# A transformer block with expert retrieval on one core: a fourth gather buffer, rows turned step by step, whole ada tiles, norms by inverse root

## The chip, the core and the metric

The kernel runs on one core of a Trainium2 chip. Its engines run side by side, each through its own instructions in order: TensorE (PE in the profile; PEld is its weight load), VectorE (DVE), ScalarE (ACT), GpSimd (POOL) and SyncE (SP), which only issues DMAs here. DMA queues: q1 carries what SyncE issues, q10 what ScalarE issues, q0 what GpSimd issues (the gathers). The metric is the device time of one execution in microseconds (us), as the median of several runs. A profiled execution is one more run, taken with the hardware profiler.

## The reference

One block of a streaming encoder, 512 tokens of 2048 features, all in fp32:

```python
mod = jax.nn.silu(c) @ ada_w[l] + ada_b[l]
sh1, sc1, gt1, sh2, sc2, gt2 = [m[:, None, :] for m in jnp.split(mod, N_ADA, axis=-1)]
h = rmsnorm(x, norm1_g[l]) * (1.0 + sc1) + sh1
x = x + gt1 * token_mixer(h, ...)
h = rmsnorm(x, norm2_g[l]) * (1.0 + sc2) + sh2
x = x + gt2 * peer_ffn(h, ...)
return rmsnorm(x, final_norm_g)

def rmsnorm(x, g):
    y = x * lax.rsqrt(jnp.mean(x * x, axis=-1, keepdims=True) + EPS)
    return y * g

def peer_ffn(h, w_q, sub_keys, u_tab, v_tab):
    ...
    act = jax.nn.gelu(jnp.einsum('td,tkd->tk', h_b, u_tab[i_b]))
    return jnp.einsum('tk,tkd->td', g_b * act, v_tab[i_b])
```

In `peer_ffn` eight heads pick 16 of 16384 experts each (`idx`, with weights `g`). So each token uses 128 experts, rows of two tables u and v of 16384 x 2048.

## The kernel before

**First half.** `ada_lead` multiplies silu(c) into the shift and scale columns of `ada_w`. It loads tiles `araw` of 128 x 1024 floats, six buffers, on SyncE, and accumulates them into `adacc` on VectorE (line 201), a few of them on TensorE (`prow`). It does so in five pieces of columns (`PIECES`), and the input projection of a piece (`plk`, `plead`, `pgl`) begins when its h is made (`h_hi`, `h_lo`, lines 257 to 259). A weight tile `raw` is split by ScalarE and VectorE into `hi` and `lo`, and three matmuls (lines 129 to 131) make one product. `rstd_from` (line 211) makes the inverse root of a mean square: a square root on ScalarE, a reciprocal on VectorE, one Newton step. It serves four norms of 128 x 512: the first, the two small ones of the attention ranks, and the second (`rs2`).

**Expert half.** Tokens 176 to 511 (336 of them, `TD`) go through all 16384 experts densely: 128 chunks of 128 experts, in 32 groups of four. For a chunk, `u_chunk` makes `pu` (two weight tiles `raw<-in_u_t`, 48 matmuls), a gelu, and `make_w` multiplies by the routing weights `gg` and `gl`, read back from DRAM (`g_d`, `gl_d`), into `wh` and `wl`. `v_slice` then multiplies with the v rows into `pvv` (two tiles `raw<-in_v_t`, 48 matmuls), and VectorE adds that to `acc` (line 1207). The first 32 chunks have their `pu` made earlier (`lead_chunk`, while routing runs) and kept in DRAM (`act_d`): these "old" groups come last and have only v matmuls.

**Gathered tokens.** Tokens 0 to 127 and 48 more gather their rows instead: `fetch` (line 984) starts an indirect DMA of 128 rows of 8 KB into a buffer `gt` (tag "gat"); VectorE multiplies it with h (`use_u`, line 990) or adds it to a sum (`use_v`, lines 1000 and 1002). The 48 are two sets, x (32 tokens) and y (16), laid out so that each gather fills 128 partitions; `build_h` lays out their h by four copies, sixteen transposes and four evacuations (`h2r` and `ph2x`, `h2s` and `ph2y`). There are 352 gathers. `gather_to` starts them at a steady rate per sub-step (`sub`: 16 in a group with u and v, 8 in an old one), each tied to the last matmul placed ahead of it:

```python
if len(landing) == GLAG:
    use_one()
landing.append((use, fetch(tab, ix, k), k, args, post))
```

`x_done` runs after the last gather of set x: it stores `accs["x"]` to `gx_d` and calls `build_h("y")`, whose result takes the same buffer (tag "hX", one buffer).

**Order.** A scheduler places each engine's instructions by priority, mostly in the order in which the code is written; `hi` and `lo` are raised. SyncE issues all weight tiles, ada tiles and gg loads in one order, and a DMA that waits for its buffer holds those behind it.

## Time and profile before

| | |
|---|---|
| median of 3 runs | 3721.33 us (3717.72 to 3724.13) |
| the profiled execution | 3719.46 us, span 3717.7 us |
| TensorE busy | 3568.5 us (96%) |
| VectorE busy | 2887.9 us (78%) |
| ScalarE busy | 1360.4 us (37%) |
| DMA | 962.75 MB, mean 259 GB/s |
| q1 / q0, share of 16 DMA engines' span | 42.5% / 26.6% |

Busy time is a sum over stages with different limits, so the table by itself doesn't say where time can be saved. A wait is read as "who waited <- who ended it". Idle time counts for the kernel's end only where it is on the engine that the stage waits for. The granted clock is the share of TensorE's full speed (2.4 GHz) that it was given over a stretch: it has two levels, 1.2 and 2.4 GHz.

### The profile page before, as it was taken

How to read it: one execution, taken by the hardware profiler on the slowest of the kernel's cores; microseconds unless marked ns; L12 is line 12 of the kernel's file. 1: busy time of each engine (PE TensorE's matmuls, PEld its weight loads, DVE VectorE, ACT ScalarE, POOL GpSimd, SP SyncE). 2: the span in 40 equal slices, each digit the busy share in tenths (PEclk: the TensorE clock that was granted, in tenths of full speed). 3: DMA queues.
4: the chain of work that ended last, by engine and by line, in shares of the span. 5: the costliest groups of instructions: out<-in, count | busy, mean ns of one | idle time of the engine just before them, and what ended most of it. 6: DMA issues, size and time to landing. Idle time of an engine off the chain costs nothing.

```text
span 3717.7 us, 52118 instructions
## 1 busy us (share of the span) xinstructions
PE 3568.5 (96%) x20165; PEld 3207.0 (86%) x20165; DVE 2887.9 (78%) x4315; ACT 1360.4 (37%) x1942; POOL 488.2 (13%) x399
## 2 busy tenths in 40 slices
PE   7999999999999989999999999999998999998888
PEld 4776778888788878889999999999998999998878
DVE  7866675455344348999988999999898998999877
ACT  3243335555422234235653333333333333332233
POOL 0000000000000000000112222222222222223400
PEclk9999999999999999999999999999999999999999
DMA  9746655544444443246789999999998999999874
GB/s 307 251 142 205 194 182 167 162 158 146 129 145 136 137 121 97 90 138 212 288 327 371 369 375 372 383 374 376 368 377 325 377 366 358 371 380 354 311 271 147
DMA packets 280824, 962.75 MB, mean 259 GB/s; under 512 B 25672, under 2 KB 76872, under 8 KB 233424
## 3 DMA queue, kind: packets, MB, share of 16 engines
q1 hardware_dynamic: 203184, 533.84, 42.5%
q0 software_dynamic: 52272, 391.14, 26.6%
q10 hardware_dynamic: 25120, 34.44, 2.7%
q8 instruction: 158, 2.59, 0.3%
q14 instruction: 90, 0.74, 0.1%
HBM read 913.26 MB, written 46.01 MB: 258 GB/s over the span
## 4 chain that ended last, share of the span: by engine, by line
PE 75%; DVE 14%; DMA 8%; issue 2%; ACT 1%; ACTq 0%; DVEq 0%; SPq 0%; POOLq 0%
PE pvv L129 6%; PE pvv L131 6%; PE pvv L130 6%; PE pu L131 5%; PE pu L130 5%; PE pu L129 5%; PE proj L129 4%; PE proj L131 4%; PE proj L130 4%; DVE lo L115 2%; DMA raw<-in_u_t 2%; PE pbr L131 2%; PE pbr L129 2%; PE pbr L130 2%; DMA raw<-in_v_t 2%
## 5 line engine op out<-in xcount | busy, mean ns | idle before, releaser
L129 PE MATMUL pvv<-wh,hi 128*128 128x336 f32 x2048 | 653.9, 319 | 39.2 <-DVE acc L1207 37.5
L131 PE MATMUL pvv<-wh,lo 128*128 128x336 f32 x2048 | 654.2, 319 | 2.5 <-DVE lo L1316 2.5
L130 PE MATMUL pvv<-wl,hi 128*128 128x336 f32 x2048 | 654.2, 319 | 0.0
L114 ACT ACTIVATE hi<-raw 128x1024 fp32r<-128x1024 f32 x288 | 304.6, 1059 | 576.3 <-PE pu L130 179.6
L129 PE MATMUL pu<-h2c_hi,hi 128*128 128x336 f32 x1536 | 487.8, 318 | 13.6 <-ACT hi L114 7.0
L131 PE MATMUL pu<-h2c_hi,lo 128*128 128x336 f32 x1536 | 489.6, 319 | 8.7 <-DVE lo L115 8.6
L130 PE MATMUL pu<-h2c_lo,hi 128*128 128x336 f32 x1536 | 487.5, 317 | 0.0
L129 PEld LDWEIGHTS pvv<-wh,hi 128*128 128x128 f32 x2048 | 389.4, 190 | 46.7 <-issue 36.9
L1315 ACT ACTIVATE hi<-raw 128x1024 fp32r<-128x1024 f32 x256 | 271.1, 1060 | 427.1 <-PE pu L130 176.1
L117 ACT ACTIVATE hi<-raw 128x1024 fp32r<-128x1024 f32 (+2 forms) x193 | 201.8, 1046 | 594.0 <-PE proj L130 164.2
L115 DVE TENSOR_TENSOR lo<-raw,hi 128x1024 fp32r<-128x1024 f32 x288 | 350.8, 1218 | 61.4 <-ACT hi L114 53.7
L131 PEld LDWEIGHTS pvv<-wh,lo 128*128 128x128 f32 x2048 | 391.4, 191 | 5.2 <-DVE lo L1316 5.0
L130 PEld LDWEIGHTS pvv<-wl,hi 128*128 128x128 f32 x2048 | 389.8, 190 | 0.0
L984 POOL DMA_INDIRECT gt<-in_u,idx x128 | 160.9, 1257 | 1703.1 <-PE pg L1091 1318.2
L118 DVE TENSOR_TENSOR lo<-raw,hi 128x1024 fp32r<-128x1024 f32 (+2 forms) x193 | 232.7, 1206 | 155.9 <-ACT hi L117 146.3
L1316 DVE TENSOR_TENSOR lo<-raw,hi 128x1024 fp32r<-128x1024 f32 x256 | 311.8, 1220 | 28.8 <-ACT hi L1315 28.3
L1002 DVE SCALAR_TENSOR_TENSOR acca<-gt,wk,acca 128x2048 f32<-128x2048 f32 x127 | 297.9, 2346 | 19.4 <-DMA gt<-in_v,idx 19.2
L990 DVE SCALAR_TENSOR_TENSOR gt<-gt,h2nat 128x2048 f32<-128x2048 f32 x128 | 292.5, 2287 | 24.3 <-DMA gt<-in_u,idx 23.8
L129 PEld LDWEIGHTS pu<-h2c_hi,hi 128*128 128x128 f32 x1536 | 290.5, 189 | 15.3 <-ACT hi L114 8.3
L131 PEld LDWEIGHTS pu<-h2c_hi,lo 128*128 128x128 f32 x1536 | 290.1, 189 | 12.8 <-DVE lo L115 12.7
L160 DVE SCALAR_TENSOR_TENSOR adacc<-raw,silc,adacc 128x512 f32<-128x512 f32 x240 | 180.0, 750 | 143.5 <-DMA raw<-in_ada 139.7
L130 PEld LDWEIGHTS pu<-h2c_lo,hi 128*128 128x128 f32 x1536 | 290.7, 189 | 0.0
(357 smaller groups left out, 7206.0 us busy)
## 6 DMA issues: line engine op xcount, KB each, us to landing
raw<-in_u_t SPq DMA_DIRECT2D x256, 512.0 KB, 7.6
raw<-in_v_t SPq DMA_DIRECT2D x256, 512.0 KB, 7.5
raw<-in_ada SPq DMA_DIRECT2D x128, 512.0 KB, 4.0
araw<-in_ada SPq DMA_DIRECT2D x64, 512.0 KB, 6.3
raw<-in_w_gate SPq DMA_DIRECT2D x44, 512.0 KB, 3.7
g_d<-stg POOLq DMA_DIRECT2D x10, 2048.0 KB, 10.6
gg<-g_d SPq DMA_DIRECT2D x16, 1280.0 KB, 17.3
raw<-in_w_out SPq DMA_DIRECT2D x32, 512.0 KB, 4.5
```

The costliest lines, as they stand in the source:

```text
L114: SC.activation(hi[:, :n], raw[:, :n], AF.Copy)
L115: VE.tensor_sub(lo[:, :n], raw[:, :n], hi[:, :n])
L117: SC.activation(hi[:, :n], raw[:, :n], AF.Copy)
L118: VE.tensor_sub(lo[:, :n], raw[:, :n], hi[:, :n])
L129: TE.matmul(out, w[0], x[0], start=first, stop=False, **kw)
L130: TE.matmul(out, w[0], x[1], start=False, stop=False, **kw)
L131: last_mm[0] = TE.matmul(out, w[1], x[0], start=False, stop=last, **kw)
L160: VE.scalar_tensor_tensor(acc[:], r, silc[:, j:j + 1], acc[:], op0=ALU.mult, op1=ALU.add)
L990: pace(VE.scalar_tensor_tensor(t[:], t[:], 1.0, h()[:], op0=ALU.mult, op1=ALU.mult, accum_out=dt[:, k:k + 1]), mybir.DependencyClass.NoSync)
L1002: ins = VE.scalar_tensor_tensor(accs[nm][:], t[:], w[:, k:k + 1], accs[nm][:], op0=ALU.mult, op1=ALU.add)
L1315: SC.activation(hi[:], raw[:], AF.Copy)
L1316: VE.tensor_sub(lo[:], raw[:], hi[:])
```

## The change

Five edits. `NGAT` goes from 3 to 4 and `GLAG` from 2 to 3: four gather buffers, and a gather is read three gathers after it was started instead of two. `build_h` becomes a generator `h_steps`, one of whose five steps runs per lead chunk (set x) or per sub-step (set y, after six sub-steps of nothing). The ada tiles come from a copy of the same weights laid out tile by tile (`ada_l`), so a tile is one contiguous 512 KB. `rstd_from` takes the inverse root on ScalarE and has no reciprocal; the final norms in `scale_out` are left as they are. `load_g` loads the routing weights of one group where it loaded those of two, into buffers half as large.

```diff
--- before.py
+++ after.py
@@ -39,8 +39,8 @@
 M0 = 1
 PIECES = [(0,2),(2,4),(4,8),(8,12),(12,16)]
 NEG = -3.0e38
-NGAT = 3
-GLAG = 2
+NGAT = 4
+GLAG = 3
 NEARLY = 20
 CI, CT, CM, CR, CO, CF = 0, 128, 256, 384, 512, 640
 NCONST = 641
@@ -178,6 +178,9 @@
         VE.tensor_add(mod[:, v, 4 * q:4 * q + 4], pst[:, 0:4], adab[:, v, 4 * q:4 * q + 4])
         yield
 
+    def lead_tile(d0, d1, u):
+        return 2 * d0 + u
+
     def ada_lead(d0, d1, pool, sil2, npe):
         w = (d1 - d0) * 128
         cols = slice(d0 * 128, d1 * 128)
@@ -188,7 +191,7 @@
             acc = ap.tile([128, 512], F32, name="adacc", tag="adacc", bufs=2)
             for u in range(16 // nj):
                 raw = pool.tile([128, 1024], F32, name="araw", tag="araw", bufs=NARAW)
-                SY.dma_start(raw[:].rearrange("p (j c) -> p j c", j=nj), a["ada"][v, :, nj * u:nj * u + nj, cols])
+                SY.dma_start(raw[:], a["ada_l"][v, lead_tile(d0, d1, u)])
                 for jj in range(nj):
                     j = nj * u + jj
                     r = raw[:, jj * w:jj * w + w]
@@ -211,8 +214,7 @@
 
     def rstd_from(pss, out, n, tmp):
         VE.tensor_scalar(tmp[0], pss, 1.0 / n, EPS, op0=ALU.mult, op1=ALU.add)
-        SC.activation(tmp[1], tmp[0], AF.Sqrt)
-        VE.reciprocal(out, tmp[1])
+        SC.activation(out, tmp[0], AF.Abs_reciprocal_sqrt)
         VE.scalar_tensor_tensor(tmp[0], tmp[0], -0.5, out, op0=ALU.mult, op1=ALU.mult)
         VE.tensor_mul(tmp[0], tmp[0], out)
         VE.scalar_tensor_tensor(out, tmp[0], 1.5, out, op0=ALU.add, op1=ALU.mult)
@@ -772,7 +774,7 @@
             SC.activation(sq[:], x1T[:, d, :], AF.Square)
             if d == 15:
                 warm = Op.tile([128, 1], F32, name="warm")
-                SC.activation(warm[:], sq[:, 0:1], AF.Sqrt)
+                SC.activation(warm[:], sq[:, 0:1], AF.Abs_reciprocal_sqrt)
             VE.tensor_add(ssum[:], ssum[:], sq[:])
     VE.scalar_tensor_tensor(a2[:], mod[:, 4, :], 1.0, g2, op0=ALU.add, op1=ALU.mult)
     for d in range(6):
@@ -1004,21 +1006,36 @@
 
     hx = {}
 
-    def build_h(nm, tmp, psum):
+    def h_steps(nm, tmp, psum):
         r0, n = sets[nm][0:2]
         hx[nm] = gr.tile([128, D], F32, name="h2" + nm, tag="hX", bufs=1)
-        for j in range(4):
+
+        def copy(j):
             h2r = tmp()
             src = h2xT[:, 4 * j:4 * j + 4, None, r0:r0 + n].to_broadcast([128, 4, 128 // n, n])
             pin(VE.tensor_copy(h2r[:].rearrange("p (i q t) -> p i q t", i=4, t=n), src))
+            return h2r
+
+        def turn(j, h2r):
             pb = psum()
             for i in range(4):
                 pin(TE.transpose(pb[:, i * 128:i * 128 + 128], h2r[:, i * 128:i * 128 + 128], ident))
             SC.activation(hx[nm][:, j * 512:j * 512 + 512], pb[:], AF.Copy)
 
+        h2r = copy(0)
+        for j in range(4):
+            yield
+            turn(j, h2r)
+            if j < 3:
+                h2r = copy(j + 1)
+
+    later = []
+
     def x_done():
         SC.dma_start(gx_d[:], accs["x"][:])
-        build_h("y", lambda: Ep_[0].tile([128, 512], F32, name="h2s"), lambda: psu_[0].tile([128, 512], F32, name="ph2y", tag="pu", bufs=2))
+        gen = h_steps("y", lambda: Ep_[0].tile([128, 512], F32, name="h2s"),
+                      lambda: psu_[0].tile([128, 512], F32, name="ph2y", tag="pu", bufs=2))
+        later.extend([None] * 6 + [gen] * 5)
 
     Ep_, psu_ = [None], [None]
     gat = [("u", idx, k, use_u, (lambda: h2nat, dots, wk, g0), None) for k in range(128)]
@@ -1105,7 +1122,9 @@
             nb += 1
         gather_to(NEARLY * (c - NL0 + 1) // (NLEAD - NL0))
         if c == NL0 + 5:
-            build_h("x", lambda: Gp.tile([128, 512], F32, name="h2r", tag="h2r", bufs=2), lambda: bank("ph2x"))
+            hgen = h_steps("x", lambda: Gp.tile([128, 512], F32, name="h2r", tag="h2r", bufs=1), lambda: bank("ph2x"))
+        if c >= NL0 + 5:
+            next(hgen, None)
     PO.close("Gp")
     PO.close("Rp")
     PO.close("ps")
@@ -1137,19 +1156,21 @@
         steps[0] += 1
         if fin[0] is not None:
             next(fin[0], None)
+        if later:
+            gen = later.pop(0)
+            if gen is not None:
+                next(gen, None)
         gather_to(NEARLY + -(-(len(gat) - NEARLY) * steps[0] // (nsub - 33)))
 
     def load_g(g):
-        if g % 2:
-            return
-        t = Ep.tile([128, NW, 256], F32, name="gg", tag="gg", bufs=2)
-        tl = Ep.tile([128, 8 * WL], F32, name="gl", tag="gl", bufs=2)
-        SY.dma_start(t[:], g_d[:, :, 128 * g:128 * g + 256].rearrange("b p c -> p b c"))
-        SY.dma_start(tl[:], gl_d[:, 4 * WL * g:4 * WL * (g + 2)])
-        gtiles[g // 2] = t, tl
+        t = Ep.tile([128, NW, 128], F32, name="gg", tag="gg", bufs=2)
+        tl = Ep.tile([128, 4 * WL], F32, name="gl", tag="gl", bufs=2)
+        SY.dma_start(t[:], g_d[:, :, 128 * g:128 * g + 128].rearrange("b p c -> p b c"))
+        SY.dma_start(tl[:], gl_d[:, 4 * WL * g:4 * WL * (g + 1)])
+        gtiles[g] = t, tl
 
     def make_w(e2, at, tie=False):
-        g, c = divmod(e2, 8)
+        g, c = divmod(e2, 4)
         t, tl = gtiles[g]
         av = at[:, :32 * NW].rearrange("p (b t) -> p b t", t=32)
         ins = VE.tensor_mul(av, av, t[:, :, c * 32:c * 32 + 32])
@@ -1370,6 +1391,14 @@
     col = lambda n: f(n).reshape(-1, 128).T
     o["vecs"] = c(np.concatenate([f("c").reshape(128, 16), adab, col("norm1_g"), col("norm2_g"), col("mla_q_norm_g"),
                                   col("mla_kv_norm_g")], axis=1))
+    ada = f("ada_w")[0].reshape(128, 16, 6, 2048)
+    tiles = []
+    for d0, d1 in PIECES:
+        w = (d1 - d0) * 128
+        nj = 1024 // w
+        p = ada[:, :, 0:2, d0 * 128:d1 * 128].reshape(128, 16 // nj, nj, 2, w)
+        tiles.append(p.transpose(3, 1, 0, 2, 4).reshape(2, 16 // nj, 128, 1024))
+    o["ada_l"] = c(np.concatenate(tiles, axis=1))
     o["ada"] = c(f("ada_w")[0].reshape(128, 16, 6, 2048).transpose(2, 0, 1, 3))
     o["ada_b"] = c(f("ada_b").reshape(1, -1))
     w = f("w_in")[0]
```

Three places show how the order of instructions moves. The first is VectorE at the second norm; `n` and `rs` are the mean square and its inverse root, `hn` and `h_lo` the first chunks of the normed rows. Before:

```order
L776 TENSOR_TENSOR ssum<-ssum,sqo 128x512
L213 TENSOR_SCALAR n_9671<-pss_9668 128x512
L215 RECIPROCAL rs_9670<-n_9672 128x512
L216 SCALAR_TENSOR_TENSOR n_9671<-n_9671,rs_9670 128x512
L217 TENSOR_TENSOR n_9671<-n_9671,rs_9670 128x512
L218 SCALAR_TENSOR_TENSOR rs_9670<-n_9671,rs_9670 128x512
L257 SCALAR_TENSOR_TENSOR hn<-x1T,a_88,rs_9670 128x512 x2
L259 SCALAR_TENSOR_TENSOR h_lo<-hn,mod,h_hi 128x512 x2
```

After:

```order
L778 TENSOR_TENSOR ssum<-ssum,sqo 128x512
L216 TENSOR_SCALAR n_9668<-pss_9665 128x512
L218 SCALAR_TENSOR_TENSOR n_9668<-n_9668,rs_9667 128x512
L219 TENSOR_TENSOR n_9668<-n_9668,rs_9667 128x512
L220 SCALAR_TENSOR_TENSOR rs_9667<-n_9668,rs_9667 128x512
L259 SCALAR_TENSOR_TENSOR hn<-x1T,a_88,rs_9667 128x512 x2
L261 SCALAR_TENSOR_TENSOR h_lo<-hn,mod,h_hi 128x512
```

The reciprocal is gone, and the first `h_lo` stands after two `hn` as it did.

The second is VectorE in the expert half, where set y's h is laid out; `h2s` are the copies, `acca` a gather's use, `lo` the weight tiles. Before:

```order
L1162 TENSOR_TENSOR wl<-at,wh 128x336
L1013 COPY h2s<-h2xT 128x512
L1002 SCALAR_TENSOR_TENSOR acca<-gt,wk,acca 128x2048
L1013 COPY h2s<-h2xT 128x512
L1316 TENSOR_TENSOR lo<-raw,hi 128x1024
L1013 COPY h2s<-h2xT 128x512
L1207 TENSOR_TENSOR acc<-acc,pvv 128x672
L1013 COPY h2s<-h2xT 128x512
L1207 TENSOR_TENSOR acc<-acc,pvv 128x672
L1002 SCALAR_TENSOR_TENSOR acca<-gt,wk,acca 128x2048
L1316 TENSOR_TENSOR lo<-raw,hi 128x1024
```

After:

```order
L1016 COPY h2s<-h2xT 128x512
L1228 TENSOR_TENSOR acc<-acc,pvv 128x672
L1183 TENSOR_TENSOR wl<-at,wh 128x336
L1004 SCALAR_TENSOR_TENSOR acca<-gt,wk,acca 128x2048
L1337 TENSOR_TENSOR lo<-raw,hi 128x1024
L1016 COPY h2s<-h2xT 128x512
L1228 TENSOR_TENSOR acc<-acc,pvv 128x672
L1016 COPY h2s<-h2xT 128x512
L1337 TENSOR_TENSOR lo<-raw,hi 128x1024
L1004 SCALAR_TENSOR_TENSOR acca<-gt,wk,acca 128x2048 x2
L115 TENSOR_TENSOR lo<-raw,hi 128x1024
L1016 COPY h2s<-h2xT 128x512
```

The four copies stood within seven rows, with one weight tile and one gather's use among them. Now they span twelve, with three weight tiles and three uses, and all of it stands six sub-steps after the end of set x's sum.

The third is SyncE at the start of the expert half's main loop; `gg` and `gl` are the routing weights, `raw` the weight tiles. Before:

```order
L1147 DMA gg<-g_d 128x10x256
L1148 DMA gl<-gl_d 128x128
L109 DMA raw<-in_u_t 128x1024 x2
L1147 DMA gg<-g_d 128x10x256
L1313 DMA raw<-in_v_t 128x1024 x2
L1148 DMA gl<-gl_d 128x128
L109 DMA raw<-in_u_t 128x1024 x2
```

After:

```order
L1168 DMA gg<-g_d 128x10x128
L1169 DMA gl<-gl_d 128x64
L1168 DMA gg<-g_d 128x10x128
L1169 DMA gl<-gl_d 128x64
L109 DMA raw<-in_u_t 128x1024 x2
L1334 DMA raw<-in_v_t 128x1024 x2
L109 DMA raw<-in_u_t 128x1024 x2
L1334 DMA raw<-in_v_t 128x1024
L1168 DMA gg<-g_d 128x10x128
L1169 DMA gl<-gl_d 128x64
L1334 DMA raw<-in_v_t 128x1024
```

The first two groups' weights stood in one load and now stand in two, both ahead of the next weight tiles; after that a load stands in each group, of half the columns, instead of one in every second group.

## Rows read from the trace of the kernel before

**Rows 1.** Busy time by stretch: us and instructions per engine, granted clock, DMA

```profile
0.00:42.50 42.50, 23.98 (x64) 9.99 (x64) 21.27 (x46) 15.97 (x25) 0.21 (x4) 0.89 0.96 319
...
1962.00:3382.00 1420.00, 1391.91 (x8956) 1382.11 (x8955) 1319.81 (x1301) 476.07 (x584) 379.43 (x298) 0.99 0.96 370
2796.00:2812.00 16.00, 7.74 (x30) 6.43 (x31) 9.41 (x11) 3.34 (x5) 1.94 (x1) 0.57 0.68 269
3382.00:3579.00 197.00, 160.96 (x956) 158.24 (x957) 167.64 (x175) 51.04 (x60) 64.59 (x30) 0.90 0.85 318
```

**Rows 2.** Timeline of the first norm: start, duration, instruction, idle before and its end

```profile
26.76 3.35 DVE L215 RECIPROCAL rs<-n 128x512 f32<-128x512 f32 x1
...
37.21 1.01 PE L203 MATMUL prow<-adacc,sil 128*2 128x256 f32 x2 [7.09 <-DVE adacc L201]
...
42.51 1.65 PE L129 MATMUL plk<-h_hi,hi 128*128 128x512 f32 x3 [2.81 <-ACT h_hi L258]
```

**Rows 3.** Timeline of the second norm, VectorE and TensorE

```profile
1378.21 3.35 DVE L215 RECIPROCAL rs<-n 128x512 f32<-128x512 f32 x1 [0.69 <-ACT n L214]
...
1386.05 0.80 PE L129 MATMUL pwq<-h_hi,hi 128*128 128x512 f32 x1 [8.61 <-ACT h_hi L258]
```

**Rows 4.** TensorE's waits, 1962 to 3382 us: total, times, longest

```profile
PE pu L131 <- DVE lo L115: 7.0, 11, 1.0
PE pu L129 <- ACT hi L114: 7.0, 4, 3.1
PE ph2y L1016 <- ACT h2y L1017: 5.4, 1, 5.4
PE ph2y L1016 <- DVE h2s L1013: 4.1, 2, 2.8
```

**Rows 5.** Waits of TensorE and of VectorE, 3382 to 3579 us

```profile
PE pvv L129 <- DVE acc L1207: 36.3, 11, 8.9
...
DVE acca L1002 <- DMA gt<-in_v,idx: 9.2, 2, 5.4
DVE accy L1002 <- DMA gt<-in_v,idxy: 8.0, 2, 5.1
```

**Rows 6.** SyncE's waits, 0 to 150 us

```profile
SPq L191 <- DVE adacc L201: 52.4, 28, 5.5
```

**Rows 7.** Timeline of ScalarE, 2785 to 2815 us

```profile
2795.75 0.33 ACTq L1020 DMA_DIRECT2D gx_d<-accx  x1
...
2807.31 1.09 ACT L1017 ACTIVATE h2y<-ph2y 128x512 f32<-128x512 f32 x2 [10.08 <-DMA gx_d<-accx]
```

**Rows 8.** DMA issues: count, KB each, median us from issue to landing

```profile
raw<-in_u_t SPq DMA_DIRECT2D x256, 512.0 KB, 7.6
...
gg<-g_d SPq DMA_DIRECT2D x16, 1280.0 KB, 17.3
```

**Rows 9.** The chain that ended last, in order of time: start, duration

```profile
3006.57 17.42 DMA raw<-in_u_t
```

**Rows 10.** DMA queues: pieces, MB, share; 3007 to 3009, then 3010 to 3012 us

```profile
q0 software_dynamic: 87, 0.70, 83.1%
q1 hardware_dynamic: 94, 0.16, 21.1%
...
q1 hardware_dynamic: 665, 0.68, 101.5%
```

**Rows 11.** Timeline of TensorE at the main loop's first group

```profile
1956.45 0.65 PE L129 MATMUL pu<-h2c_hi,hi 128*128 128x336 f32 x1 [5.93 <-ACT at L1169]
```

**Rows 12.** Timeline of GpSimd and VectorE around one late gather

```profile
3444.43 5.28 POOL L984 DMA_INDIRECT gt<-in_v,idx  x1 [7.52 <-DVE wl L1162]
...
3458.93 2.35 DVE L1002 SCALAR_TENSOR_TENSOR acca<-gt,wk,acca 128x2048 f32<-128x2048 f32 x1 [5.38 <-DMA gt<-in_v,idx]
...
3462.75 2.34 DVE L1002 SCALAR_TENSOR_TENSOR acca<-gt,wk,acca 128x2048 f32<-128x2048 f32 x1
```

## The prediction

> **What bounds the kernel now.** I read the stretches first [rows 1]. From 1962 to 3382 us, the main stretch of the expert stage, TensorE is busy for 1391.9 of 1420 us, VectorE for 1319.8, and the DMA engines are in use for 0.96 of it: three resources are near full, and the most that can be won is TensorE's idle 28.1 us. From 3382 to 3579 us, where the old groups run with gathers, TensorE idles 36.0 us of 197 and VectorE 29.4; here VectorE is the busier one. The 16 us around 2796 hold 30 matmuls and 7.7 us of busy TensorE at a granted clock of 0.57. In the first 42.5 us TensorE is busy for 24.0. So the question for each edit is which of these holes it fills.
>
> The waits say what ends the holes. At the start TensorE waits 7.09 us for VectorE's adacc and 2.81 for h_hi [rows 2]. Before the second norm's product it waits 8.61 us [rows 3]. In the main stretch it waits for `lo`, `hi` and, in two lines of 5.4 and 4.1 us, for the turning of the second set's rows [rows 4]. In the old groups all 36.3 us are `pvv <- DVE acc`: the PSUM tile is not yet added up, because VectorE is late [rows 5].
>
> **The change part by part.**
>
> *Norms by inverse root.* Each of four [128x512] norms loses a RECIPROCAL of 3.35 us and swaps one function for another in an ACT instruction that was there before; the same number of table loads stands in ACT's order. At the second norm the reciprocal lies on the path: VectorE does it at 1378.21, TensorE starts at 1386.05 after 8.61 us idle [rows 3]. Nothing else lies beside it, so 3.3 us go. At the first norm it sits among the adacc steps that TensorE waits 7.09 us for [rows 2]; VectorE has no hole there, so the adacc chain and with it mod, h_hi and the first product move up by 3.35, if the last ada tiles have landed by then; I read no wait of VectorE for one there. I take 3.4, with 0 (the tiles become the limit) and 7 as ends. The two small norms lie in stretches where TensorE has other work: nothing.
>
> *ada tiles of one piece.* 64 loads of 512 KB, in pieces of 1 or 2 KB before, now 4 KB. That shortens each transfer, but SyncE's queue mostly waits for VectorE to release the tiles (52.4 us in 28 waits, [rows 6]): the tiles come when VectorE has room, not when DMA has. So 0. It also moves rows in SyncE's order, ada ahead of weights; if that makes TensorE wait, the cover is the idle time it has there anyway. The ends are those of the line above.
>
> *The second set's rows turned step by step.* Before, the four copies, sixteen transposes and four evacuations stand in one place, and ACT's evacuation waits 10.08 us for the store of accx, whose buffer it takes [rows 7]; TensorE waits 5.4 and 4.1 us [rows 4], and the granted clock is 0.57 [rows 1]. The 30 matmuls of those 16 us would take 30 x 0.155 (1391.9 / 8956, [rows 1]) = 4.7 us, so 11.3 are lost [rows 1]. After it six sub-steps pass before the first copy, and a sub-step in this stretch is about 3.8 us (16 in a group, 1420 us for some 23.5 groups), so some 22 us cover the 11 of the store. Each turn then costs only its transposes. A turn takes a `pu` buffer that the chunks also use, so I leave 1.3 us: 10 us go, between 5.4 (the store's wait alone) and 11.3. The first set's turns get the same treatment where no long TensorE wait stands in these rows: nothing.
>
> *Gate rows (gg) loaded per group.* This pays for the fourth buffer: 16 loads of 1280 KB become 32 of 640 KB. A load was 10 x 128 = 1280 pieces of 1 KB and is now 1280 pieces of 512 B, so the pieces double in all. What hurts today is that the weight tiles queue behind a gg load on SyncE's queue: gg lands after 17.3 us in the median, a weight tile after 7.6 [rows 8], and one behind gg after 17.42 [rows 9]. TensorE's idle time in the main stretch, less the 9.5 us of the turning, is 18.6 us; 11 gg loads fall in it, 1.7 us each. How long will a half load hold the queue? While a gather is under way its 8 KB pieces and the 1 KB pieces pass about one for one (87 against 94 in 2 us); with no gather there, 665 pass in 2 us [rows 10]. So the paired part of a load keeps its length, and the part between gathers goes by bytes and shrinks by up to half. Today gg adds 9.8 us to a weight tile (17.42 less 7.6), and the worst wait is 3.1 [rows 4], so landing by about 14.3 costs nothing. If a half load adds half to two thirds of 9.8, the tile lands after 12.5 to 14.1. I take 0.45 us of stall a load, for the spread: 23 x 0.45 = 10.4 instead of 18.6, 8 us gained. The ends are 18.6 gained (no stall left) and 20.5 lost (each of 23 loads stalls 1.7 as now).
>
> The very first gg load, on which TensorE waits 5.93 us [rows 11], has gathers beside it for most of its time, and now a second load stands behind it ahead of the weights. I take 1.5, between 0 and 5.
>
> The Trainium skill (DMA: Bandwidth & Descriptors, Queues, rings and completion order) says that each DMA engine takes turns between the queues that have work and switches at whole packets. By that rule alone a gg load beside steady gathers would take as many turns as before, and the sum would lose 20.5 here where I gain 8. The trace agrees on the turns (87 against 94) and shows too that the gathers leave holes [rows 10].
>
> *Four gather buffers, read three gathers later.* A gather is issued where it was: POOL's order is the same, each still paced by the matmul ahead of it and by VectorE's use one step earlier. But it is read one gather later. In the main stretch VectorE's waits on gathers cost TensorE almost nothing, so I count none. In the old groups VectorE waits 9.2 + 8.0 = 17.2 us for gathers in four places [rows 5]. The worst was issued at 3444.43, with 5.28 us in POOL's issue, and used at 3458.93 after 5.38 us of waiting; the next use begins 3.82 us later, at 3462.75 [rows 12]. One step more leaves 1.6 us of the 5.38, 1.3 of the 5.1, and nothing of the others: 2.9 remain, 14.3 go. VectorE is the limit of that stretch (167.6 of 197 busy), so its saving is the kernel's: 14. The ends are 3 (below) and 29.4 (all of VectorE's idle time). Next late there is VectorE itself.
>
> The sum: 3.3 + 3.4 + 10 + 8 + 1.5 + 14 = 40.2 us. The profiled execution took 3719.46, so 3679.3; the median of the runs is 1.9 above it: **3681 us**.
>
> **The rivals.** *Short pieces cost as much as long ones.* For it: one for one in [rows 10]; against it: the holes between gathers, where 665 pass in 2 us. Every gg load then stalls 1.7 us, now 23 of them: 3681 + 8 + 20.5 = 3709.5 us. The skill's rule named above gives this time.
>
> *Slower: the gathers fill the holes.* With a third gather under way the gathers' queue may never be empty, a gg load goes through in paired turns only, and all weight tiles behind it come late in every group. The price is at least the worst wait of today, 3.1 us [rows 4], in each of 23 groups: 71.3 against 18.6, a loss of 52.7, so 3681 + 8 + 52.7 = 3742 us. It decides from (40.2 - 8 + 18.6) / 23 = 2.2 us a load on. Against it: the issue of gathers is tied to matmuls, so as many are under way as before.
>
> *The change does not do what it says in the old groups.* The late gathers are late because POOL issues late and slowly while VectorE streams (5.28 us, [rows 12]); with VectorE denser, POOL may be held longer, and the wait moves one gather on. Then 3 us go instead of 14: 3692 us.
>
> **How the numbers follow.** Forecast 0.56, old groups unmoved 0.20 (3692), short pieces 0.14 (3709.5), slower 0.07 (3742), others 0.03. The forecast's own terms reach from 3657 (main stretch 18.6, old groups 22) to 3695. With the first two rivals the range is 3657 to 3712, which leaves out the slower case and what lies beyond either end. A measurement of this kernel can tell about 0.2% (7.4 us) from no change. Faster than that: the forecast, the first rival listed at 3692 and most of the one at 3709.5, 0.86; within it 0.06; slower 0.08.
>
> **What would show it.** Right: no RECIPROCAL before the second norm's product and about 5.3 us idle there; no `ph2y` wait over 2 us and no half clock at 2800; gathers' waits of VectorE in the old groups under 5 us in all and that stretch near 183 us; gg landing under 14 us, weight tiles behind it near 12. Wrong: weight tiles behind gg landing at 16 us or more in every group, or a new wait of POOL for a buffer. What would upset all of it is TensorE idling over 40 us in the main stretch.

## The result, and the profile after

| | before | after |
|---|---|---|
| median | 3720.82 us (3717.72 to 3724.13, 4 runs) | 3658.64 us (3655.00 to 3660.81, 4 runs) |
| span of the profiled execution | 3717.7 us | 3653.2 us |
| ratio of times | | 0.9832, 95% interval 0.9815 to 0.9849 |

The change wins 62 us. The forecast was 40 us, 3681; the time lies inside the range, 1.6 us above its lower end. So the sign was right and the size was not, and the question is where 22 us more came from.

The page of the changed kernel, first the engines' busy time, then groups of instructions (busy time, mean ns of one, idle time before them and who ended it):

```profile
PE 3545.2 (97%) x20165; PEld 3195.5 (87%) x20165; DVE 2877.0 (79%) x4311; ACT 1359.6 (37%) x1942; POOL 708.8 (19%) x399
...
L1004 DVE SCALAR_TENSOR_TENSOR acca<-gt,wk,acca 128x2048 f32<-128x2048 f32 x127 | 297.7, 2344 | 3.5 <-DMA gt<-in_v,idx 3.4
...
L992 DVE SCALAR_TENSOR_TENSOR gt<-gt,h2nat 128x2048 f32<-128x2048 f32 x128 | 291.8, 2284 | 2.2 <-DMA gt<-in_u,idx 2.2
```

VectorE does the same work (2887.9 us before). What is gone is idle time: its uses of gathered rows now wait 3.5 and 2.2 us in all. TensorE executes the same 20165 matmuls in 23 us less busy time, with its mean granted clock at 0.991 instead of 0.984.

To see where the 64.5 us of span went, I cut both spans at the same points of the program: the first matmul of a stage. "Group n" is the first `pvv` matmul of group n, counted from 0 in the order of running. Group 23 is the last new one, of which only v matmuls are left, as of the old ones.

| stretch | before | after | won | forecast |
|---|---|---|---|---|
| start to the first product (`plk`) | 42.5 | 38.8 | 3.7 | 3.4 |
| attention ranks to the gates (`pqn` to `pz`) | 286.9 | 289.7 | -2.8 | 0 |
| second norm's sum to its product (`pss2` to `pwq`) | 10.4 | 6.3 | 4.1 | 3.3 |
| the rest of the way to group 0 | | | 3.3 | 1.5 |
| group 0 to group 22, main stretch | 1343.5 | 1307.4 | 36.1 | 18 |
| group 23 to group 28, old groups with gathers | 197.1 | 170.7 | 26.4 | 14 |
| group 28 to the end | 150.6 | 157.0 | -6.4 | 0 |

(0.1 us between groups 22 and 23 makes the sum 64.5.) The early terms add up to what was forecast. Both late terms are about twice as large, and 6.4 us are given back at the end.

Busy time over the main stretch and the old groups, in both kernels (columns: start:end, length, busy us and count of PE, PEld, DVE, ACT, POOL, granted clock, DMA share, GB/s). Before:

```profile
1974.70:3318.20 1343.50, 1315.92 (x8466) 1306.76 (x8465) 1244.83 (x1232) 448.96 (x550) 357.45 (x281) 0.99 0.96 370
3370.00:3567.10 197.10, 161.73 (x962) 158.73 (x961) 168.94 (x179) 50.47 (x60) 67.54 (x32) 0.90 0.88 330
```

After:

```profile
1966.40:3273.80 1307.40, 1303.71 (x8466) 1303.16 (x8465) 1247.65 (x1233) 449.31 (x550) 542.85 (x281) 1.00 0.98 380
3325.50:3496.20 170.70, 152.72 (x962) 149.78 (x961) 165.06 (x173) 50.13 (x59) 92.36 (x32) 0.98 0.97 362
```

In the main stretch TensorE's idle time fell from 27.6 to 3.7 us, and its busy time by another 12.2 us for the same 8466 matmuls, with the granted clock at 1.00 instead of 0.99. In the old groups idle fell from 35.4 to 18.0 and busy by 9.0, with the clock at 0.98 instead of 0.90. Behind the stall of 3.12 us that ends at 3025.2 us, for one, the granted clock before is 0.66 over the next 4.8 us. So about a third of both gains is time that matmuls spent at the lower level, 1.2 GHz, around the stalls. The prediction counted idle time alone.

TensorE's waits of [rows 4] are gone but for one; the only one left from 1966 to 3274 us (us in total, times, longest):

```profile
PE ph2y L1022 <- DVE h2s L1016: 3.6, 1, 3.6
```

In the old groups and the group behind them (3318 to 3540 us) the wait of [rows 5] is smaller, and VectorE's waits for gathers have all but vanished; a wait for `act_d` has taken their place:

```profile
PE pvv L129 <- DVE acc L1228: 24.4, 11, 6.4
...
DVE at L1179 <- DMA at<-act_d: 9.2, 4, 3.5
...
DVE acca L1004 <- DMA gt<-in_v,idx: 0.4, 1, 0.4
```

### The profile page after: what moved, and what is told of

The parts are those of the page before. It is cut to its first block, busy times and chain, and to the rows that moved or that the text cites. A ratio compares the mean times of both kernels' runs of the same rounds, so it can differ in the third digit from the quotient of the medians.

```text
span 3653.2 us, 52112 instructions
## 1 busy us (share of the span) xinstructions
PE 3545.2 (97%) x20165; PEld 3195.5 (87%) x20165; DVE 2877.0 (79%) x4311; ACT 1359.6 (37%) x1942; POOL 708.8 (19%) x399
## 4 chain that ended last, share of the span: by engine, by line
PE 85%; DVE 10%; DMA 3%; issue 1%; ACT 1%; ACTq 0%; DVEq 0%; SPq 0%; POOL 0%; POOLq 0%
PE pvv L129 8%; PE pvv L130 8%; PE pvv L131 8%; PE pu L131 6%; PE pu L130 6%; PE pu L129 6%; PE proj L129 4%; PE proj L131 4%; PE proj L130 4%; DVE lo L115 2%; PE pbr L131 2%; PE pbr L129 2%; PE pbr L130 2%; PE pwo L129 2%; PE pwo L131 2%; PE pwo L130 2%
## 5 line engine op out<-in xcount | busy, mean ns | idle before, releaser
L129 PE MATMUL pvv<-wh,hi 128*128 128x336 f32 x2048 | 650.0, 317 | 24.5 <-DVE acc L1228 24.4
L986 POOL DMA_INDIRECT gt<-in_u,idx x128 | 211.4, 1652 | 1636.3 <-PE pg L1108 1310.8
L986 POOL DMA_INDIRECT gt<-in_v,idx x128 | 285.1, 2227 | 321.0 <-PE pu L131 96.0
```

The source lines that it names most:

```text
L129: TE.matmul(out, w[0], x[0], start=first, stop=False, **kw)
L986: ins = GP.indirect_dma_start(out=t[:], out_offset=None, in_=a[tab], in_offset=bass.IndirectOffsetOnAxis(ap=ix[:, k:k + 1], axis=0))
```

## Experiments

All kernels below start from the changed one. Times are medians; the kernel before, timed beside them, was at 3714 to 3722 us.

### Which edit freed the main stretch: buffers and reading, or the gate rows

The prediction gave the main stretch to the half gg loads and nothing to the gathers there. Two kernels were written to take one of the two away each; only the first does.

**Three gather buffers, read two gathers later, gg still per group.**

```diff
-NGAT = 4
-GLAG = 3
+NGAT = 3
+GLAG = 2
```

> Three gather buffers, read two gathers later, as before; all other edits stay, gg one group at a time. Theory A (two causes: the half gg loads freed the main stretch, the later reading freed the old groups): groups 1 to 14 of the main stretch stay at 59.1 us each with no TensorE wait for lo or hi, and the old groups from the 24th to the 29th go back from 170.7 us to about 197, with some 17 us of VectorE's waits for gathers; of these 26 us the 6.5 that the next group gave back return, so about 3678 us. Theory B (the later reading freed both): main groups of 60 to 65 us come back as well, some 27 us more, about 3705 us. Theory C (neither: the gain of the old groups is the gg's too): 3659 us.

Measured: 3682.48 us, ratio to before 0.9901 (0.9864 to 0.9938). Its main stretch and its old groups:

```profile
1966.80:3285.40 1318.60, 1307.60 (x8465) 1302.69 (x8465) 1243.57 (x1232) 448.97 (x550) 371.14 (x281) 1.00 0.98 376
3337.30:3532.90 195.60, 162.09 (x963) 159.08 (x962) 169.09 (x179) 50.46 (x60) 69.97 (x32) 0.90 0.89 329
```

The old groups are back to within 1.5 us of before, and with them 15.1 us of VectorE's waits for gathers (17.2 in [rows 5]):

```profile
DVE accy L1004 <- DMA gt<-in_v,idxy: 8.4, 2, 4.4
DVE acca L1004 <- DMA gt<-in_v,idx: 6.7, 2, 3.7
```

The main stretch stands in between: 11.2 us longer than the changed kernel's, 24.9 shorter than before. Its groups take 59.1 to 61.4 us (67.4 at the turning), so Theory A comes nearest, with something of B. TensorE's waits for `lo` and `hi` there are 6.0 us, where before they were 18.1 (14.0 of it in [rows 4]):

```profile
PE pu L131 <- DVE lo L115: 4.9, 8, 2.1
...
PE pvv L131 <- DVE lo L1337: 1.1, 4, 0.5
```

**gg in half loads, written two of them back to back in every second group; four buffers as changed.**

```diff
     def load_g(g):
-        t = Ep.tile([128, NW, 128], F32, name="gg", tag="gg", bufs=2)
-        tl = Ep.tile([128, 4 * WL], F32, name="gl", tag="gl", bufs=2)
+        if g % 2 == 0:
+            load_one(g)
+            load_one(g + 1)
+    def load_one(g):
+        t = Ep.tile([128, NW, 128], F32, name="gg", tag="gg", bufs=3)
+        tl = Ep.tile([128, 4 * WL], F32, name="gl", tag="gl", bufs=3)
```

> The gg rows in the same half loads of 512 B pieces, but two of them back to back in every second group, as one burst with 1280 KB as before. Theory A (what hurt was the length of the burst ahead of the weight tiles): every second group of the main stretch is 60 to 65 us again and the others 59.1, TensorE waits for lo and hi some 20 to 27 us in all there, and the time is 3680 to 3690 us; with twice the pieces in a burst it may be worse than before, up to 3700. Rival (four buffers read later take the stall out, whatever the burst): all groups stay at 59.1, 3659 us.

Measured: 3660.24 us, ratio 0.9839 (0.9804 to 0.9875), no different from the changed kernel. Its main stretch (its old groups take 171.3 us):

```profile
1970.80:3280.20 1309.40, 1304.79 (x8467) 1303.17 (x8466) 1246.75 (x1235) 449.47 (x550) 526.77 (x281) 1.00 0.99 380
```

But the trace shows that the edit did not make the bursts. The two loads stand side by side in the code, and SyncE still issues one load per group, some 60 us after the last, as in the changed kernel. Two in a row:

```profile
2077.99 0.39 SPq L1173 DMA_DIRECT2D gg<-g_d  x1
...
2139.92 0.41 SPq L1173 DMA_DIRECT2D gg<-g_d  x1
```

So this kernel is the changed one with a third gg buffer. Its equal time says nothing of bursts, neither for the theory nor for the rival. That leaves three of four cases for the main stretch:

| | gathers read two later | read three later, four buffers |
|---|---|---|
| gg in 1280 KB, every second group | 1343.5 | not run |
| gg in 640 KB, each group | 1318.6 | 1307.4 |

From the kernel before to the one with three buffers 24.9 us go. Two edits act there. The turning is worth 6.5 us when it is undone alone (below), and 8.9 us from group 13 to group 15 between before and after. The half loads are left with 16.0 to 18.4. From there, reading later wins 11.2. What reading later would win with full loads no run shows, so it stays open whether the two gains depend on each other.

How both delays reach TensorE can be read from the chain that ended last. Some of its pieces, start and length in us; before, 3120 to 3150:

```profile
3120.66 2.21 DVE gt L990 x2
3122.87 1.14 DVE lo L115
...
3125.53 2.29 DVE gt L990 x2
3127.82 0.92 DVE lo L115
3128.99 18.44 DMA raw<-in_u_t
```

VectorE reads two gathers between its `lo` steps; each `lo` gives a weight buffer back, and SyncE issues the next tile only then. The tile then needs 18.44 us behind a gg load, issued at 3124.43. So the tile is late by both. In the kernel with three buffers the five longest pieces of that chain from 1976 to 3270 us are gathers, two of them:

```profile
2007.81 11.44 DMA gt<-in_u,idx
...
2443.46 11.52 DMA gt<-in_u,idxx
```

VectorE's waits for gathers in the main stretch, which the prediction set aside, were 38.7 us before (1975 to 3318 us), 6.6 of it in lines left out here:

```profile
DVE lo L115 <- ACT hi L114: 26.2, 8, 5.7
DVE gt L990 <- DMA gt<-in_u,idx: 16.4, 14, 3.6
DVE lo L1316 <- ACT hi L1315: 11.6, 10, 3.6
DVE acca L1002 <- DMA gt<-in_v,idx: 9.1, 11, 1.8
DVE gt L990 <- DMA gt<-in_u,idxx: 6.6, 6, 2.4
```

After, they are 5.2 us. Its waits for `lo` are as long in all, but in 52 short ones where there were 18:

```profile
DVE lo L115 <- ACT hi L114: 25.8, 34, 4.4
DVE lo L1337 <- ACT hi L1336: 12.7, 18, 2.4
...
DVE gt L992 <- DMA gt<-in_u,idx: 2.2, 2, 1.2
DVE acca L1004 <- DMA gt<-in_v,idx: 1.5, 1, 1.5
```

VectorE has time to spare in this stretch in both kernels (98.7 us idle before, 59.8 after). Before, it spent much of that waiting for gathers, and came late to the next weight tile; now it waits for weight tiles, and comes at once when one lands. A wait for a gather is not by itself a stall of TensorE: with three buffers and half loads VectorE waits 51.2 us for gathers there, more than before, and that stretch is only 11.2 us longer than the changed kernel's.

**Four buffers, read two later.**

```diff
 NGAT = 4
-GLAG = 3
+GLAG = 2
```

> Four gather buffers, but each gather read two gathers later as before. Theory A (the later reading is what counts, since a gather was read before it had landed): VectorE's waits for gathers in the old groups return, about 17 us, and the time is that of the kernel with three buffers, about 3678 us. Rival (the spare buffer is what counts: the issue on GpSimd no longer waits for VectorE to release one): waits stay below 3 us and the time is 3659 us.

Measured: 3685.42 us, ratio 0.9908 (0.9873 to 0.9944), as with three buffers. Its main stretch takes 1320.7 us and its old groups 195.6. In the main stretch GpSimd waits mostly for the matmul that paces it. Its waits for VectorE to use a gathered row and so release a buffer fall to 41.2 us, from 414.7 before (133.2 in the changed kernel). Before, the largest of its waits was:

```profile
POOL gt L984 <- DVE gt L990: 277.6, 79, 10.3
```

VectorE's waits for gathers in the old groups stay, 15.3 us. So the spare buffer frees GpSimd's issue of this wait, and that alone wins nothing. The later reading is the cause; the buffer is what makes it possible.

### The second set's turning

**All turns in one place again.**

```diff
-        later.extend([None] * 6 + [gen] * 5)
+        for _ in gen:
+            pass
```

> The second set's rows turned in one place again, all else as changed. Theory A (the copies and evacuations in one place wait for the store of accx): the group of the turning goes from 66.4 back to about 75.3 us, TensorE's waits for ph2y of some 9 us and the half clock near 2800 return, 3667 us. Rival (what is left there, 7.3 us, comes from the weight tile that is late behind the gg load and the store, and the turning itself costs nothing): the group stays within 2 us of 66.4 and the time within 3 us of 3659.

Measured: 3661.55 us (3657.75 to 3670.89), which the timing can't tell from 3658.64. In the trace the group of the turning takes 72.9 us instead of 66.4, and the waits of [rows 7] and [rows 4] are there again:

```profile
ACT h2y L1023 <- DMA gx_d<-accx: 12.1, 1, 12.1
...
PE ph2y L1022 <- ACT h2y L1023: 6.3, 1, 6.3
```

So by the trace the step by step turning is worth 6.5 us in this kernel. The changed kernel still loses 7.3 us there, against a group of 59.1; its chain:

```profile
2789.78 12.18 DMA raw<-in_u_t
...
2803.15 1.22 DVE lo L115
2804.46 0.35 DVE h2s L1016
2804.85 1.12 PE ph2y L1022 x4
```

A copy `h2s` stands behind a `lo` whose tile landed late, and TensorE stands at the transposes behind it, although it has other products to make.

**The store in four parts, the turns six sub-steps behind the last** (on top of the final rows' edit below).

```diff
-        SC.dma_start(gx_d[:], accs["x"][:])
+        def stores():
+            for j in range(4):
+                SC.dma_start(gx_d[:, 512 * j:512 * j + 512], accs["x"][:, 512 * j:512 * j + 512])
+                yield
...
-        later.extend([None] * 6 + [gen] * 5)
+        later.extend([st_] * 4 + [None] * 6 + [gen] * 5)
```

> As the kernel before this one in the list (final rows on the gathers' queue), and the store of accx to gx_d in four parts, one per sub-step, with the turns six sub-steps behind the last. Theory (the 7.3 us left at the second set's turning come from a weight tile that is late behind the store and the gg load): the group there falls from 66.4 to 60 to 61 us, 5 to 6 us less than the kernel before it, about 3647 us. Rival (the turning's copies cost VectorE the time wherever they stand): it stays at 65 to 67 us, the same time as the kernel before it.

Measured: 3658.82 us; the group takes 69.1 us. ScalarE waits 9.6 us for the weight tile there, longer than the 6.9 us of the changed kernel.

The theory fell: with the store spread, the tile behind the gg load is still late, and the group is longer than the rival said too. ScalarE waits for such tiles in other groups as well (70.2 us in 23 waits over the changed kernel's main stretch); why the longest wait is this one was not found.

### The norms and the ada tiles

**All four norms with square root and reciprocal.**

```diff
-        SC.activation(out, tmp[0], AF.Abs_reciprocal_sqrt)
+        SC.activation(tmp[1], tmp[0], AF.Sqrt)
+        VE.reciprocal(out, tmp[1])
```

> All four norms with square root and reciprocal again, all else as changed. Theory (the sum's terms: 3.3 us at the second norm, 3.4 at the first): TensorE's idle time before the second norm's product is about 8.6 us again instead of 4.5, the first product of the attention ranks starts 3.4 us later, and the time is about 3665 us, or 3662 if the small norms won back the 2.8 us that the stretch from 272 to 562 us lost. Rival (the first norm's gain comes from the ada tiles of one piece, not from the norm): the start stays at 38.8 us and only the second norm is dearer, 3662 us.

Measured: 3662.9 us (3659.45 to 3666.96). TensorE's idle time before the second norm's product is 8.12 us:

```profile
1383.85 0.80 PE L129 MATMUL pwq<-h_hi,hi 128*128 128x512 f32 x1 [8.12 <-ACT h_hi L261]
```

In the changed kernel it is 4.51, where [rows 3] have 8.61:

```profile
1381.02 0.50 PE L129 MATMUL pwq<-h_hi,hi 128*128 128x512 f32 x1 [4.51 <-ACT h_hi L260]
```

At the start its wait for `adacc` is 6.9 us; in the changed kernel it is 3.6. Both differences are about one reciprocal (3.35 us). The first product starts at 41.1 us, 2.3 later than after and 1.4 earlier than before. 1.0 of that 1.4 lies ahead of the norm: VectorE's first step of it (`n<-pss`), which waits for TensorE's sum, begins at 24.45 us before, 24.40 after and 23.48 here.

**Only the ada tiles strided again.**

```diff
-                SY.dma_start(raw[:], a["ada_l"][v, lead_tile(d0, d1, u)])
+                SY.dma_start(raw[:].rearrange("p (j c) -> p j c", j=nj), a["ada"][v, :, nj * u:nj * u + nj, cols])
```

> Only the ada tiles come in strided pieces of 1 or 2 KB again. Theory (the tiles wait for VectorE to release them, not for DMA; the first norm alone gave the 3.7 us at the start): the first product of the attention ranks starts at 38.8 us as it does now, the time stays within 2 us of 3659. Rival (the tile of one piece gave a part: with the old norms the start went back only to 41.1, not to 42.5): it starts at 40.2 us or later, some 1.4 us lost, up to 3661.

Measured: the first product starts at 38.9 us and group 0 at 1965.7 (1966.4 in the changed kernel): nothing lost up to there. The time was 3663.5 us (3657.71 to 3669.73); what its profiled execution loses comes behind group 0, in groups that this edit doesn't reach, so I take it for the spread of this kernel, without proof. The last 0.4 us between 41.1 and 42.5 stay unexplained.

**Only the two small norms with square root and reciprocal.**

```diff
-        rstd_from(p2[:], r[:], 128 * n, (tm[0][:], tm[1][:]))
+        rstd_old(p2[:], r[:], 128 * n, (tm[0][:], tm[1][:]))
```

> Only the two small norms of the attention ranks with square root and reciprocal, the first and the second norm as changed. Theory (the inverse root there loads a table on ScalarE between steps that TensorE waits for, and so lost the 2.8 us): the stretch from the first query-rank product to the next stage's falls from 289.7 to about 287 us, the time to 3656 us. Rival (those 2.8 us are other work's spread, not the norms'): that stretch stays between 288 and 291 us, the time within 2 us of 3659.

Measured: 3658.64 us, the same as the changed kernel, so the timing doesn't show the gain. In the trace the stretch from `pqn` to `pz` is 286.9 us, that of before, where the changed kernel has 289.7, and group 0 begins 2.2 us earlier. The cause is not a table load: from 268 to 300 us ScalarE makes one in either kernel. ScalarE's instructions stand in another order. In the changed kernel (282 to 289 us; the brackets hold the idle time ahead and who ended it):

```profile
285.76 1.06 ACT L117 ACTIVATE hi<-raw 128x1024 fp32r<-128x1024 f32 x1 [5.82 <-DMA raw<-in_w_gate]
286.73 0.58 ACT L320 ACTIVATE rx<-pqr 128x512 f32<-128x512 f32 x1
```

With the small norms as before:

```profile
283.13 0.60 ACT L328 ACTIVATE rx<-pqr 128x512 f32<-128x512 f32 x1 [2.84 <-PE pqr L544]
284.78 1.06 ACT L117 ACTIVATE hi<-raw 128x1024 fp32r<-128x1024 f32 x1 [1.05 <-DMA raw<-in_w_gate]
```

With the shorter norm the scheduler puts a split `hi` ahead of the evacuation of `pqr`. The split waits 5.82 us for its weight tile, and TensorE waits behind both:

```profile
287.36 2.08 PE L322 MATMUL prot<-rx,cst 128*128 128x512 f32 x2 [3.69 <-ACT rx L320]
```

### The old groups and the end

**The final rows (fgb, gt2b, x1, gx) on the gathers' queue.**

```diff
-            SC.dma_start(rows[name][:], src.partition_broadcast(128))
+            GP.dma_start(rows[name][:], src.partition_broadcast(128))
```

(and the three loads of `x1`, `gx` and `x1x` in the same way)

> As changed, but the final rows (fgb, gt2b, x1, gx) are loaded on the gathers' queue, not on ScalarE's, where the old chunks' act_d tiles come. Theory (the 6.5 us given back in the group after the last gather are VectorE's waits for act_d behind those loads): that group falls from 39.0 to about 33 us, VectorE's waits for act_d from 9.2 to about 3, the time to 3652 us. Rival (the loads compete for the same DMA engines whichever queue they stand in): that group stays at 38 to 39 us, 3659 us.

Measured: 3660.35 us. The group after the last gather falls from 39.0 to 35.5 us, but TensorE's waits for `acc` from 3300 to 3560 us are 25.2 us in all, against 24.4 before that edit, and VectorE still waits 7.3 us for `act_d`. The five groups ahead take 180.0 us instead of 170.7, in a profiled execution that was the slowest of the four. So another queue for those loads wins nothing; the 6.4 us given back are not explained by it.

**More gathers into the main stretch:** they end two old groups earlier, and in a second kernel before the old groups.

```diff
-        gather_to(NEARLY + -(-(len(gat) - NEARLY) * steps[0] // (nsub - 33)))
+        gather_to(NEARLY + -(-(len(gat) - NEARLY) * steps[0] // (nsub - 49)))
...
-        if i == NG - 4:
+        if i == NG - 6:
```

> As changed, but the gathers are started at a slightly higher rate, so that the last comes 16 sub-steps (two old groups) earlier, and the work on the gathered tokens' rows begins two groups earlier. Theory (the old groups are bound by VectorE, 165.1 of 170.7 us busy against TensorE's 152.7, while the main stretch has 62 us of VectorE idle): some 13 gathers' 2.35 us move out of the old groups, TensorE's 24 us of waiting for acc there shrink to 8 to 12, main groups stay at 59.1, and the time is 3643 to 3648 us. Rival (the main stretch has no room: its DMA engines are in use for 0.99 of it, so more gathers there bring back late weight tiles): main groups of 60 to 62 us, a gain under 5 us or a loss up to 15 us, 3654 to 3674.

> The same with all gathers ended before the old groups, 32 sub-steps earlier. Theory of VectorE as the bound of the old groups: no wait for acc there but those of the rows' last work, the five groups together near 5 x 30 us instead of 170.7, but 59 us more of VectorE's work in the main stretch than now, where 62 are idle: its groups begin to stall, so 3635 to 3650 us. Rival (no room on the DMA engines in the main stretch): it loses there more than it gains, 3660 to 3690 us.

(The second has 65 and 8 in place of 49 and 6.) Measured: 3668.36 and 3692.0 us. The main stretch of the first:

```profile
1966.20:3281.60 1315.40, 1308.04 (x8466) 1304.03 (x8466) 1267.61 (x1245) 448.77 (x551) 430.27 (x293) 1.00 0.99 387
```

And of the second:

```profile
1966.30:3320.40 1354.10, 1319.70 (x8466) 1306.16 (x8465) 1292.49 (x1251) 447.91 (x549) 399.94 (x304) 0.99 0.99 384
```

23 more gathers in the main stretch cost it 46.7 us, 2.0 each, although VectorE still has 61.6 us idle. The DMA engines are in use for 0.99. VectorE hardly waits for gathers there (1.1 us), it waits for weight tiles: 34.5 us for those of u and 27.9 for those of v, from 1970 to 3350 us.

So both times came out as the rival said (the second 2 us above its range): the changed kernel's main stretch has no room for the gathers left to the old groups. That it is the DMA engines that have none is read from their share and from these waits, and not shown by itself: most of TensorE's own waits there are for VectorE's `acc`, 20.1 of 33.8 us.

**The last gathers read one per sub-step, and the small norms as before.**

```diff
-        gather_to(NEARLY + -(-(len(gat) - NEARLY) * steps[0] // (nsub - 33)))
+        if begun[0] == len(gat) and landing:
+            use_one()
+        gather_to(NEARLY + -(-(len(gat) - NEARLY) * steps[0] // (nsub - 37)))
```

> As changed, with two edits: the two small norms with square root and reciprocal again, and the last gathers started four sub-steps earlier and read one per sub-step instead of all at once. Theory (VectorE's run of four 2.34 us sums near 3503 to 3511 us makes TensorE's 6.4 us of waiting for acc at 3515; the small norms cost 2.8 us in the stretch from 272 to 562): that stretch is 286.9 us, the group from the 28th to the 29th falls from 39.0 to about 35.5, and the time is some 6 us below the changed kernel's, 3652 to 3654 us. Rival (VectorE's work is only moved, and TensorE waits for it a group earlier): the groups from the 26th to the 29th take together what they take now, 105.4 us, and the time is 3656 to 3659.

Measured: 3649.18 us (3645.93 to 3654.78, 5 runs), ratio to before 0.9809 (0.9789 to 0.9829). This is 9.5 us below the changed kernel, more than expected. The two were not timed side by side, and the intervals of their ratios overlap (0.9815 to 0.9849 for the changed one); their profiled spans differ by 5.8 us (3647.4 and 3653.2). The stretch from `pqn` to `pz` is 285.4 us, group 28 to group 29 takes 29.5 instead of 39.0, the five groups ahead of it 174.7 instead of 170.7. TensorE's waits there (3300 to 3560 us):

```profile
PE pvv L129 <- DVE acc L1238: 20.0, 11, 3.5
```

The longest is 3.5 us, where it was 6.4. That wait came behind a run of gathers that are read at once when the last has been started. Two of them on VectorE, in the changed kernel (others stand at 3489.18 and 3506.53 us):

```profile
3503.13 2.34 DVE L1004 SCALAR_TENSOR_TENSOR accy<-gt,wky,accy 128x2048 f32<-128x2048 f32 x1
...
3509.19 2.34 DVE L1004 SCALAR_TENSOR_TENSOR accy<-gt,wky,accy 128x2048 f32<-128x2048 f32 x1
```

The six groups together take 204.2 us instead of 209.7. So most of the 6.4 us given back was probably this; a lag of three leaves one more gather for that run than a lag of two. How the 9.5 us divide between the two edits was not timed; by the traces, 2.8 to 4.3 lie at the small norms.

## Why the prediction came out as it did

**Norms.** Right: 4.1 us at the second norm (3.3 forecast), 3.7 at the start (3.4), each about one reciprocal by the kernel with the old norms. "The two small norms ... nothing" failed: they lost 2.8 us, by ScalarE's order and not by their own length.

**ada tiles.** Right, 0, at the place where they act. "I read no wait of VectorE for one there" was not quite so: before, VectorE waits 0.16 us for one at 34.83 us, and 0.55 after at 34.19, too little to count.

**Turning.** Forecast 10; from group 13 to group 15 it won 8.9 us (134.4 us before, 125.5 after), and 6.5 when undone alone. The expected sign "no `ph2y` wait over 2 us" was wrong: one of 3.6 us is left, from a late tile and not from the store. "No half clock at 2800" came true in part: the granted clock is 0.89 from 2796 to 2812 us (0.57 before), and 0.66 from 2804 to 2809.

**Main stretch.** The mechanism named for the half loads held, and three steps failed. First, "VectorE's waits on gathers cost TensorE almost nothing, so I count none": they were 38.7 us, some of them stood ahead of the `lo` steps that release weight buffers, and reading later is worth 11.2 us there on top of the half loads. Second, the half loads were mis-sized: 8 us forecast, 16.0 to 18.4 measured, near the upper end of 18.6. Third, that upper end was idle time alone. With the stalls went 12.2 us of busy TensorE too, so the whole stretch won 36.1 where the two terms' upper ends add up to 29.9. "A gather is issued where it was" did not hold either (GpSimd's waits for VectorE's release fell from 414.7 to 133.2 us), but the kernel with four buffers read two later shows that this by itself wins nothing. On landing the forecast was good: the first gg lands after 12.26 us on the chain (14.93 before), and the one weight tile behind a gg load that is left there after 12.18 (17.42 in [rows 9]), where 12.5 to 14.1 was forecast.

The rival "short pieces cost as much as long ones" asked for 1.7 us of stall in each of 23 loads. It is refuted: with half loads and three buffers TensorE waits 6.0 us for `lo` and `hi` in the whole stretch, in the changed kernel not at all. Its time is also what the Trainium skill's rule (DMA: Bandwidth & Descriptors, Queues, rings and completion order) gives by itself, that an engine takes turns between queues by packets. The turns are still there behind the changed kernel's gg load at 2013.51 us: in the 2 us from 2020 on 135 pieces of SyncE's queue pass beside 94 of the gathers' (q0), and in a hole between gathers, from 2018 to 2020, 1012 pass:

```profile
q1 hardware_dynamic: 1012, 0.62, 100.8%
...
q0 software_dynamic: 94, 0.76, 95.4%
q1 hardware_dynamic: 135, 0.07, 13.2%
```

So both parts of the prediction's picture, turns and holes, stand after the change.

**"Slower: the gathers fill the holes."** It didn't come at the changed kernel's rate. The two kernels with more gathers show that a loss of this kind begins right above: 12 more cost the main stretch 8.0 us, 23 more 46.7.

**Old groups.** The step was right, "the gathers' waits under 5 us": 0.4 us. The term was mis-sized, 26.4 where 14 was forecast. TensorE's idle time there fell by 17.4 us and its busy time by 9.0, as the clock rose from 0.90 to 0.98, and the second part had no place in the sum. "Next late there is VectorE itself" was right as well, with 165.1 of 170.7 us busy, and it gave 6.4 us back after the last gather. The rival that the wait only moves one gather on is refuted.

## What to carry to other kernels

Where a stage's engine works in order, waits that cost it nothing by themselves (VectorE has time to spare) still delay whatever stands behind them, here the release of weight buffers; price them by what they hold, not by the waiting engine's load. An experiment's time counts only if its trace shows that the edit did what it was written to do: the kernel written to load gg in pairs issued one load per group, and its time tests nothing. And a stall's price is its idle time and the matmuls at the low clock around it; count both from rows of the same stage.

## What was not expected of the hardware

GpSimd's issue of a gather got longer, from 1243 to 1738 ns (`in_u`) and from 1287 to 2117 (`in_v`) in the main stretch, with the same work on VectorE (1247.7 us busy, 1244.8 before). Main stretch after:

```profile
L986 POOL DMA_INDIRECT gt<-in_v,idx x101 | 213.8, 2117 | 262.6 <-PE pu L131 89.2 <-PE pvv L131 53.2 <-DVE wl L1183 35.8
```

Far fewer issues now begin when VectorE has just released a buffer (133.2 us of such waits, 414.7 before), so more of them begin in the midst of VectorE's work. The spare buffer goes with it: read two later, the issues take 1271 and 1377 ns with three buffers, 1526 and 1936 with four. The Trainium skill (SBUF — State Buffer, SBUF: two separate sides) says that GpSimd and VectorE share a port pair, which one instruction at a time holds whole: a VectorE operation in a two-port mode, or one with two SBUF inputs, the latter only against a GpSimd operation that reads SBUF. Most of VectorE's work here has two SBUF inputs, so the longer issues fit that only if the issue of a gather, whose row numbers lie in SBUF, is such an operation; no run here took VectorE's work away to show it.

Over the main stretch the DMA engines moved 380 to 387 GB/s at a share of 0.98 to 0.99 in the changed kernel and in those with more gathers, with pieces from 256 B (`gl`) to 8 KB, and 387 is the highest over this stretch that any kernel here reached.
